# Waits of TensorE at five stage edges of a two-layer encoder step: transposes, operand order, weights, PSUM banks and evacuations

## The chip, the cores and the metric

The kernel runs on one core of a Trainium2 chip. The metric is the time of one execution on the device in microseconds, in the median of several runs. The engines of the core are TensorE (PE in the profile, with its weight loads as PEld), VectorE (DVE), ScalarE (ACT), GpSimd (POOL) and SyncE (SP), which issues most of the DMAs. Each engine works through its own instructions in a fixed order and waits on semaphores for the others.

## The reference

One inference step of a two-layer encoder with D_MODEL = 1024, on 1024 prompt tokens and 32 sample tokens, all in float32. Layer 0 mixes tokens with a state-space model (SSD), layer 1 with latent attention; after each mixer comes a gated per-layer embedding.

```python
for i in range(DEPTH):                       # DEPTH = 2
    hn_p = rmsnorm(hp, ln_w[i]); hn_s = rmsnorm(hs, ln_w[i])
    if i % 2 == 0:
        yp, cp, sp = ssd_mixer(hn_p, conv0, h0, CHUNK, *w)
        ...
    else:
        yp, lp, rp = mla_mixer(hn_p, None, None, 0, *w)
        ...
    hp = hp + yp
    hp = hp + ple(hp, p_prompt[i], ple_up_w[i], ple_norm_w[i], ple_gate_w[i])

def ssd_mixer(...):
    proj = hn @ in_w
    z, xbc, dt = jnp.split(proj, [...])      # 2048, 4096 and 32 columns
    xbc = silu(causal_conv(xbc)); dt = softplus(dt + dt_bias)
    y, hT = ssd_scan(xs, dt, A, Bm, Cm, h0, chunk)
    y = rmsnorm_by_group((y + D * xs) * silu(z))
    return y @ out_w, ...

def ple(h, p, up_w, norm_w, gate_w):
    g = jax.nn.sigmoid(rmsnorm(h, norm_w) @ gate_w)
    return (p @ up_w) * g
```

The mixer of layer 1 projects the normed input to a query latent, a key and value latent, a rotary key and a gate (`mla_in_w`), normalises the latents, attends, multiplies by the gate and projects back (`mla_out_w`).

## The kernel before

Tokens lie in the free dimension, features in the 128 partitions. A float32 product is made of three products in the faster fp32r type: each operand is split into a rounded part (h) and the rest (l), and `gemm` (L239) sums wh·ah + wh·al + wl·ah for each block of 128 features, the k-blocks, in one PSUM bank. `load_weight` (L192) fetches a weight by SP, makes wh on ScalarE (L204) and wl on GpSimd (L205); `split` (L256) does the same for an operand on ScalarE (L258) and VectorE (L259).

The program is written with tile pools: a tile waits for its buffer, and a planner puts each engine's instructions in order by a timeline that it simulates, among those that are ready the one that stands first in the program. So the written order is a priority, and an instruction that stands later can be put ahead.

The stages and the places that matter:

- **Layer 0, heads** (`phase_ssd`, L301). The 1060 columns are treated in three pieces of 384, 384 and 292 (`TILES1`). For each piece `mblock` (L341) forms the products of three head blocks, dt (32 rows), B and C. Their results go to PSUM tiles `mm`, of which there are three; one bank each is kept for the tags trx, trb, st, yd and yf (pool `ps_c`). `raw_block` (L366) forms one further block of 128 rows with `mblock`, 72 products; its results are copied out by VectorE (L362, first piece) and ScalarE (L360).
- **dt** (L431 to L483). A chain on VectorE makes `stk` out of the dt rows (dt, its running sum, and decays); nine transposes on TensorE (L482) turn it to token rows, in banks yd, yf and st, from which VectorE copies it to `tokT` (L483). After that the pool is closed, and the pool `work` of the scan takes its place.
- **Scan** (L639 to L661). For each of 8 groups: `scan_group`, the B and C blocks of the next group, the z gates of the group before, the x blocks of the next (`x_block`), and `finish`. The transposes, products and element-wise steps of the scan use `tokT`.
- **Up products** (`up_product`, L267). For layer 0 they are formed at the end of the scan stage with weights for four blocks at a time (nb = 4): 8 blocks of 3 pieces of 352 columns, each summed in an `mm` bank by six matmuls and copied to `upe` by ScalarE (L290). For layer 1 they are formed beside the attention with nb = 1.
- **Output projections** (`phase_out`, L706), for layer 0 with 16 k-blocks and for layer 1 with 8. The 1056 columns are two halves of 528 (`HB`). For each half the operands are loaded by SP (L714, five buffers `yraw`) and split (`yhl`); then 8 blocks of 128 rows are formed. `gemm2` (L675) makes both quarters (a = 0 and 1, 264 columns, a bank each) of one half: all k-blocks for a = 0, then all for a = 1. A weight covers 8 k-blocks. The operand buffers hold about one half of layer 0, so those of the second half fall free as the first half's last products are done.
- **Gated embedding** (`phase_ple`, L759) and **input of the attention** (`phase_mla_in`, L797) use `gemm2` in the same way. The operands of the latter are what `phase_ple` gives out by `emit0` (L1468), block after block and for each half; the first block of the latter starts before the last ones are there.

## Time and profile before

| | us |
|---|---|
| median of 3 runs | 1997.85 |
| lowest and highest | 1994.87 and 1999.12 |
| the profiled execution | 1996.68 |
| its span, first to last instruction | 1994.9 |

The profile's page gives each engine's busy time, a timeline in 40 slices, the DMA queues, the chain that ended last, and the costliest groups of instructions. The trace behind it answers further questions: who waited for whom, the instructions of one engine in order of time, or busy time in chosen windows. In a group or a timeline row, `out<-in` are the program's names, and `[1.32 <-ACT raw L360]` says that the engine was idle for 1.32 us just before, until ScalarE's instruction of line 360 that writes `raw` was done. In rows by windows each engine's busy time is followed by its number of instructions, and the columns at the end are the granted clock of TensorE (1.00 is full), the share of the DMA engines and GB/s. A row that merges several instructions shows the start of the first, the time to the end of the last, and their count. Matmuls are pipelined: the pace is the distance of starts, and the time shown of one is longer.

### The profile page before, as it was taken

The page shows a single profiled execution, that of the slowest core. Times are in us where ns is not written, and L with a number is a line of the kernel's source. Part 1 is how long each engine was busy: PE and PEld are TensorE (multiplying, and loading weights), DVE is VectorE, ACT ScalarE, POOL GpSimd, SP SyncE. Part 2 cuts the span into 40 slices and gives each one's busy share as a digit, 9 for nine tenths or more (in the row PEclk, how much of TensorE's full clock was granted, in tenths as well). Part 3 has the DMA queues.
Part 4 walks back from the last instruction along what each step waited for, and adds up shares of the span by engine and source line. Part 5 has one row for each costly group of instructions (what it writes and reads, how often), then busy time and mean ns, then how long its engine had stood idle before and what let it go on. Part 6 is the DMA issues. An engine that isn't in the chain of part 4 may idle for free. (4 is left out here: it accounts for less than half of the span.)

```text
span 1994.9 us, 32715 instructions
## 1 busy us (share of the span) xinstructions
PE 1921.6 (96%) x12811; PEld 1766.3 (89%) x12811; DVE 1254.2 (63%) x1613; ACT 1051.0 (53%) x1958; POOL 955.6 (48%) x811
## 2 busy tenths in 40 slices
PE   8999999999999999999998999998999999899999
PEld 6988899999999998989998999677778777779999
DVE  7888675746657575452377443364777887976544
ACT  5436555455545557342334341777687877754331
POOL 5642524343443545555777452124445454545772
PEclk9999999999999999999999999999999999999999
DMA  4134333424233347553233221434331311316442
GB/s 141 54 86 99 87 87 104 91 78 98 74 95 88 77 119 254 161 181 122 94 125 113 84 73 69 160 107 129 78 79 43 80 40 38 121 45 199 123 130 71
DMA packets 110730, 204.26 MB, mean 102 GB/s; under 512 B 18224, under 2 KB 60720, under 8 KB 110448
## 3 DMA queue, kind: packets, MB, share of 16 engines
q1 hardware_dynamic: 105472, 193.17, 33.0%
q0 software_dynamic: 2800, 6.91, 1.8%
q8 instruction: 100, 1.64, 0.3%
q10 hardware_dynamic: 2304, 2.10, 0.3%
q14 instruction: 54, 0.44, 0.1%
HBM read 156.81 MB, written 38.83 MB: 98 GB/s over the span
## 5 line engine op out<-in xcount | busy, mean ns | idle before, releaser
L205 POOL TENSOR_TENSOR wl<-wraw,wh 128x1024 fp32r<-128x1024 f32 (+3 forms) x183 | 373.4, 2042 | 424.0 <-ACT wh L204 386.2
L245 PE MATMUL mm<-hh,wl 128*128 128x384 f32 (+1 forms) x1136 | 372.7, 328 | 0.0
L245 PE MATMUL mm<-hh,wh 128*128 128x384 f32 (+1 forms) x1136 | 372.0, 328 | 0.0
L245 PE MATMUL mm<-hl,wh 128*128 128x384 f32 (+1 forms) x1136 | 370.8, 326 | 0.0
L245 PE MATMUL pso<-yhl,wh 128*128 128x264 f32 x1536 | 282.2, 285 | 4.7 <-DVE yhl L259 2.9
L204 ACT ACTIVATE wh<-wraw 128x1024 fp32r<-128x1024 f32 (+3 forms) x181 | 157.2, 869 | 245.8 <-PE pso L245 111.6
L245 PEld LDWEIGHTS pso<-yhl,wh 128*128 128x128 f32 x1536 | 238.5, 188 | 6.2 <-DVE yhl L259 4.0
L245 PE MATMUL pso<-yhl,wl 128*128 128x264 f32 x768 | 218.6, 285 | 3.9 <-POOL wl L205 3.9
L245 PEld LDWEIGHTS mm<-hh,wh 128*128 128x128 f32 x1136 | 214.6, 189 | 3.2 <-issue 2.8
L245 PEld LDWEIGHTS mm<-hl,wh 128*128 128x128 f32 x1136 | 214.8, 189 | 1.3 <-issue 0.5
L245 PEld LDWEIGHTS mm<-hh,wl 128*128 128x128 f32 x1136 | 214.6, 189 | 0.7 <-issue 0.2
L496 DVE SCALAR_TENSOR_TENSOR cx<-raw,pv,cx 128x1060 f32<-128x1060 f32 x96 | 142.6, 1490 | 42.6 <-ACT cx L494 42.0
L245 PE MATMUL psi<-yhl,wh 128*128 128x264 f32 x832 | 154.7, 287 | 4.1 <-ACT yhl L258 3.7
L559 ACT ACTIVATE ex<-ex,tokT 128x128 f32<-128x128 f32 (+1 forms) x288 | 87.0, 380 | 132.9 <-DMA ex<-acs_d 123.8
L245 PEld LDWEIGHTS pso<-yhl,wl 128*128 128x128 f32 x768 | 144.5, 188 | 4.6 <-POOL wl L205 4.6
L245 PE MATMUL pg<-hH,wl 128*128 128x264 f32 x512 | 145.9, 285 | 1.3 <-POOL wl L205 1.3
L245 PE MATMUL pg<-hH,wh 128*128 128x264 f32 x512 | 145.9, 285 | 0.0
L245 PE MATMUL pg<-hL,wh 128*128 128x264 f32 x512 | 145.6, 285 | 0.0
L1327 PE MATMUL st<-qk 128*128 128x512 f32 (+2 forms) x576 | 139.6, 358 | 1.5 <-DMA qk<-mr 0.9
L245 PEld LDWEIGHTS psi<-yhl,wh 128*128 128x128 f32 x832 | 130.7, 190 | 5.1 <-ACT yhl L258 3.9
L1348 POOL TENSOR_TENSOR pl<-pf,ph 128x512 fp32r<-128x512 f32 x64 | 81.8, 1278 | 104.7 <-DVE ph L1347 93.8
L572 POOL TENSOR_TENSOR hm<-hT,cd_all 128x256 f32<-128x256 f32 x64 | 53.1, 830 | 162.3 <-DVE hT L574 96.1
(539 smaller groups left out, 4666.5 us busy)
## 6 DMA issues: line engine op xcount, KB each, us to landing
wraw<-in_inW SPq DMA_DIRECT2D x48, 512.0 KB, 3.5
ex<-acs_d SPq DMA_DIRECT2D x32, 512.0 KB, 5.5
wraw<-in_outW SPq DMA_DIRECT2D x32, 512.0 KB, 3.7
yraw<-y_d SPq DMA_DIRECT2D x32, 264.0 KB, 4.6
u<-u_d SPq DMA_DIRECT2D x32, 264.0 KB, 2.8
eb<-ea_d SPq DMA_DIRECT2D x64, 128.0 KB, 4.0
y_d<-y SPq DMA_DIRECT2D x16, 512.0 KB, 2.8
wraw<-in_gateW SPq DMA_DIRECT2D x16, 512.0 KB, 3.6
```

The lines of the kernel that those rows point to most:

```text
L204: nc.scalar.activation(wh, raw, AF.Copy)
L205: nc.gpsimd.tensor_tensor(wl, raw, wh.bitcast(F32), op=ALU.subtract)
L245: c.nc.tensor.matmul(ps, ww[:, k, :m], aa, start=first and k == 0 and i == 0, stop=last and k == n - 1 and i == 2)
L496: nc.vector.scalar_tensor_tensor(xh, raw[:, k : k + T1], pvc(c, "cw", 4 * b + k), xh, op0=ALU.mult, op1=ALU.add)
L559: nc.scalar.activation(e_, e_, AF.Relu, scale=-1.0, bias=tok(32)[:, i, h : h + 1])
L572: nc.gpsimd.tensor_tensor(hm.rearrange("p (h q) -> p h q", q=64), hT.rearrange("p (h q) -> p h q", q=64), bc_last(cd_all[:, hs, ch], 64), ...
L1327: nc.tensor.matmul(ps[:, :n], a_[:, ks], b_[:, q], start=t == 0, stop=t == 2)
L1348: (nc.gpsimd if idx in L_POOL else nc.vector).tensor_tensor(pl[:, :n], pf[:, :n], ph[:, :n].bitcast(F32), op=ALU.subtract)
```

## The change

Five edits:

1. `mblock` takes a list of tags. The head blocks of the second piece (j = 1) use the banks of yd, yf and trb in place of the `mm` tiles.
2. The nine transposes of `stk` get an edge for the planner alone, without a semaphore: they are put in order behind the last product of the block `x_block(1, 1)`. For that `gemm` returns its last matmul, and `mblock` notes it in `c.product`.
3. `up_product` copies the middle one of the three pieces to `upe` on VectorE where nb > 1, which holds for layer 0.
4. `gemm2` takes turns: for each k-block the three products of quarter 0, then the three of quarter 1.
5. `phase_out` loads the weights of the second half's first block (k-blocks 0 to 7) ahead of that half's operands in the program.

```diff
 def gemm(...):
         for i, (ww, aa) in enumerate(((wh, a), (wh, b), (wl, a))):
-            c.nc.tensor.matmul(ps, ww[:, k, :m], aa, start=first and k == 0 and i == 0, stop=last and k == n - 1 and i == 2)
+            p = c.nc.tensor.matmul(ps, ww[:, k, :m], aa, start=first and k == 0 and i == 0, stop=last and k == n - 1 and i == 2)
+    return p
...
 def up_product(...):
-            nc.scalar.activation(u[:, w_ * a : w_ * a + w_], ps[:, :w_], AF.Copy)
+            if nb > 1 and a % 2:
+                nc.vector.tensor_copy(u[:, w_ * a : w_ * a + w_], ps[:, :w_])
+            else:
+                nc.scalar.activation(u[:, w_ * a : w_ * a + w_], ps[:, :w_], AF.Copy)
...
-    def mblock(*blocks, ws=None, js=range(3), products=gemm):
+    def mblock(*blocks, ws=None, js=range(3), products=gemm, tags=None):
...
-            for w, (_, m, evac) in zip(ws, blocks):
-                ps = mm.tile([P, 512], F32, tag="mm", name="mm")
+            for i, (w, (_, m, evac)) in enumerate(zip(ws, blocks)):
+                ps = pc.tile([P, 512], F32, tag=tags[i], name="mm") if tags else mm.tile([P, 512], F32, tag="mm", name="mm")
...
-                    products(c, ps[:, :n], w, acts, slice(0, n))
+                    c.product = products(c, ps[:, :n], w, acts, slice(0, n))
...
     for j in range(3):
-        mblock(*heads, ws=early, js=(j,), products=gemm if j else gemm_rest_last)
+        mblock(*heads, ws=early, js=(j,), products=gemm if j else gemm_rest_last,
+               tags=("yd", "yf", "trb") if j == 1 else None)
...
+        steps = []
...
-                nc.tensor.transpose(ps[:, i], stk[:, o : o + L], c.ident[:96, :96])
+                p = nc.tensor.transpose(ps[:, i], stk[:, o : o + L], c.ident[:96, :96])
+                steps.append(p.ins)
...
             x_block(g + 1, 1)
+            if g == 0:
+
+                for p in steps:
+                    tc.add_manual_dep(p, c.product.ins.name, mybir.DependencyInfo(
+                        mybir.DependencyClass.NoSync, mybir.DependencyReason.DATA), reason="late operand")
...
-def gemm2(c, ps, w, acts, kofs=0, nk=None, m=P, first=True, last=True):
-    for a in range(2):
-        gemm(c, ps[:m, a, :264], w, acts, slice(264 * a, 264 * a + 264), m, first, last)
+def gemm2(c, ps, w, acts, first=True, last=True):
+
+    n = len(acts)
+    for k in range(n):
+        for a in range(2):
+            gemm(c, ps[:, a, :264], [x[:, k : k + 1] for x in w], acts[k : k + 1], slice(264 * a, 264 * a + 264),
+                 first=first and k == 0, last=last and k == n - 1)
...
 def phase_out(...):
         acts = []
+        ws = {}
+        if hf:
+            ws[0] = load_weight(c, W[0][:, :8], 8, P)
         for k in range(nkb):
...
-        ws = {}
-
         def part(m, a, b):
 
             u = a // 8 * 8
-            if a == u:
+            if a == u and (a or m not in ws):
                 ws[m] = load_weight(c, W[m][:, u : u + 8], 8, P)
```

## The prediction

> **What bounds the kernel now.** I read the page first, then the waits of TensorE, then its timeline around each wait, and last the other engines there.

> ```profile
> span 1994.9 us, 32715 instructions
> PE 1921.6 (96%) x12811; PEld 1766.3 (89%) x12811; DVE 1254.2 (63%) x1613; ACT 1051.0 (53%) x1958; POOL 955.6 (48%) x811
> ```

> TensorE (PE) is busy 1921.6 us of the 1994.9 us span. The change removes no product, so it can win only idle time, 73 us in all, and time at a lowered clock. The waits, cut to the rows that the edits can touch (us in total, times, longest):

> ```profile
> PE pso L245 <- POOL wl L205: 3.9, 3, 1.4
> PE pstk L482 <- issue: 3.9, 1, 3.9
> PE psi L245 <- ACT yhl L258: 3.7, 1, 3.7
> PE mm L245 <- ACT upe L290: 3.0, 2, 1.5
> PE pso L245 <- DVE yhl L259: 2.9, 3, 1.5
> PE mm L230 <- ACT raw L360: 1.3, 1, 1.3
> ```

> That is 18.7 us, the most that could be won from idle time. The clock adds to it (TensorE's busy time and matmuls first, granted clock behind POOL's column):

> ```profile
> 28.40:31.80 3.40, 1.61 (x8) 1.02 (x8) 3.40 (x5) 1.60 (x4) 2.46 (x2) 1.00 0.00 0
> 31.90:35.20 3.30, 3.30 (x13) 3.06 (x12) 2.39 (x5) 2.07 (x5) 1.84 (x2) 0.50 0.01 2
> 127.50:130.80 3.30, 3.30 (x16) 3.30 (x15) 2.86 (x7) 0.34 (x1) 0.00 (x0) 0.50 0.70 137
> 1086.70:1090.00 3.30, 3.30 (x15) 3.30 (x16) 2.62 (x2) 2.63 (x5) 3.30 (x2) 0.50 0.26 79
> ```

> After each stretch with much waiting the clock is at half for about 3.4 us, in which half the work gets done: 1.7 us lost each time. Two such stretches follow waits that the change attacks, at 127.5 and 1086.7.

> **The price of the new order of products.** `gemm2` now changes the PSUM bank after every three matmuls. Its products come from the code: 1536 and 768 in the two `phase_out`, 1488 in the two `phase_ple`, 1248 in `phase_mla_in`, together 5040. The nearest rows are the head blocks, where three tiles in three banks take turns (36 to 43 us), and an ordinary block of the same 384 columns (54 to 61 us); the third row gives the pace at 264 columns:

> ```profile
> 36.00:43.00 7.00, 7.00 (x42) 6.48 (x41) 7.00 (x10) 3.29 (x7) 5.46 (x6) 1.00 0.00 1
> 54.00:61.00 7.00, 7.00 (x42) 7.00 (x42) 5.09 (x4) 4.95 (x6) 5.48 (x11) 1.00 0.46 150
> 810.00:850.00 40.00, 40.00 (x332) 40.00 (x332) 15.81 (x10) 12.77 (x17) 22.45 (x11) 1.00 0.43 138
> ```

> 42 matmuls in 7 us both ways: I take no price. The rows can't tell one matmul in 42, that is 0.17 us / 42 = 4 ns for each, and 4 ns x 5040 = 20 us is the other end; below nothing there is no reason for one. The pace at 264 columns is 40.00 / 332 = 0.1205 us. Number and size of products and weight loads stay the same.

> **Head blocks (banks): 1.3 us.**

> ```profile
> 45.28 0.35 PE L230 MATMUL mm<-hh,whl 128*64 128x292 f32 x1 [1.32 <-ACT raw L360]
> 44.80 1.83 POOL L339 TENSOR_TENSOR hl<-hf,hh 128x292 fp32r<-128x292 f32 x2 [0.88 <-ACT hh L338]
> ```

> The third piece waits 1.32 us for a bank that ScalarE still reads. With the second piece in yd, yf and trb the third finds the three mm banks of the first piece, read long before; yd, yf and trb have no other user until the x blocks. Next late would be the last two `hl`, done at 46.63; 16 of 64 products (the two last operands of three blocks) need them, the rest cover that. The evacuations move with it, so VectorE's dt chain does too. I take 1.3; bounds 0.8 (a wait for `hl` appears) and 1.3.

> **Transposes: 4.0 us.**

> ```profile
> 126.10 0.94 PE L482 MATMUL pstk<-cst,stk 96*128 96x96 f32 x9 [3.93 <-issue]
> 126.82 0.42 PE L245 MATMUL mm<-hh,wl 128*128 128x384 f32 x1
> 131.82 0.34 PE L245 MATMUL mm<-hh,wh 128*128 128x384 f32 x1
> 124.74 1.25 DVE L477 TENSOR_TENSOR stk<-w,stk 32x1060 f32<-32x1060 f32 x1
> 132.98 1.28 ACT L559 ACTIVATE ex<-ex,tokT 128x128 f32<-128x128 f32 x4 [5.14 <-DMA ex<-acs_d]
> 150.00:205.00 55.00, 51.15 (x357) 47.30 (x356) 47.94 (x58) 34.21 (x74) 17.11 (x16) 1.00 0.40 91
> ```

> "issue" hides a wait: `stk` is finished at 124.74 + 1.25 = 125.99, and TensorE, which had nothing else first in its order, starts at 126.10. Behind the nine transposes stand the last 25 matmuls of the x block that the edit names (between the rows at 126.82 and 131.82, one of 384 columns and 24 of 292; by the 810 row in proportion to the columns 0.175 and 0.133 us): 3.4 us. They now go ahead, so the wait shrinks from 3.9 to about 0.5, and with that little idle time the half clock at 127.5 goes: 3.4 + 1.7 = 5.1 us. The transposes themselves keep their time, since they still wait for `stk`; all that is queued behind them (the copies to tokT on VectorE, the ex loads on SP, for which ScalarE then waits to 132.98) isn't later. But nor is it earlier, and from 150 to 205 TensorE is idle 3.85 us in waits on that scan. Work pulled ahead may be lacking there. I take 4.0, between 1.7 (only the clock stays won) and 5.1.

> **Evacuation of the up products: 1.4 us.**

> ```profile
> 762.44 1.28 ACT L182 ACT_TABLE_LOAD   x1
> 763.74 1.18 ACT L182 ACTIVATE yr<-yr,eps 128x1060 f32<-128x1060 f32 x1
> 765.35 0.80 ACT L290 ACTIVATE upe<-mm 128x352 f32<-128x352 f32 x2
> 766.17 1.28 ACT L183 ACT_TABLE_LOAD   x1
> 768.59 2.56 DVE L622 SCALAR_TENSOR_TENSOR y<-y,pv,yr 128x1060 f32<-128x1060 f32 x2 [2.24 <-ACT yr L183]
> ```

> Both 1.5 us waits come while ScalarE works at a table load and a long function, and three full banks wait. With every third tile read by VectorE the first wait loses the 0.4 us of one copy (0.80 / 2), as its next tile is ScalarE's; at the second one bank more is free, six matmuls (0.9 us) of slack, so 0.4 + 1.0. Two thirds of the copies stay where they were. The new copies wait in VectorE's queue: behind the L622 above, itself late by 2.24 us, one would gain nothing. Bounds 0 and 3.0.

> **Second half of the first output projection: 2.5 us.**

> ```profile
> 876.21 2.39 POOL L205 TENSOR_TENSOR wl<-wraw,wh 128x1024 fp32r<-128x1024 f32 x1 [1.66 <-ACT wh L204]
> 884.88 1.04 ACT L204 ACTIVATE wh<-wraw 128x1024 fp32r<-128x1024 f32 x1
> 888.42 0.39 PE L245 MATMUL pso<-yhl,wl 128*128 128x264 f32 x1 [1.40 <-POOL wl L205]
> 894.75 0.39 PE L245 MATMUL pso<-yhl,wh 128*128 128x264 f32 x1 [1.51 <-DVE yhl L259]
> 888.86 6.46 DVE L259 TENSOR_TENSOR yhl<-yraw,yhl 128x528 fp32r<-128x528 f32 x5
> 898.83 0.71 DVE L748 TENSOR_TENSOR hf<-pso,xres 128x528 f32<-128x528 f32 x1 [3.51 <-PE pso L245]
> ```

> The last of 16 operands is done at 888.86 + 6.46 = 895.32. Then 27 matmuls were left, 3 of the first half and 24 of the second; by turns six are left. 21 x 0.1205 = 2.5 us. The weights moved ahead are those of k-blocks 0 to 7. Their `wl` was done at 878.60, and they are in use for 48 matmuls (5.8 us) before the wait that ends at 888.42: they were on time, and moving them is worth nothing here. In the planner's order their load goes ahead of 16 operand loads in SP's queue, their copy and subtraction ahead of 16 copies on ScalarE and the sums on POOL; they need a weight buffer that falls free only as the first half ends, so I expect the same places as now, and if SP did wait for that buffer, the operand loads behind it would slip (rival 1). That wait is for k-blocks 8 to 15, whose `wh` (884.88) stands in ScalarE's queue between operand copies. Copies could now come earlier, as operand slots fall free evenly; then up to 4.5. If the planner puts that `wh` behind more copies, the gain is eaten: 0. In the other `phase_out` the late operand is a part of its own, six matmuls either way: nothing.

> **First block of the attention's input: 2.5 us.**

> ```profile
> 1085.81 0.39 PE L245 MATMUL psi<-yhl,wh 128*128 128x264 f32 x1 [3.73 <-ACT yhl L258]
> 1091.35 1.05 PE L694 MATMUL n<-acc,ones 128*128 128x264 f32 x4
> 1094.32 0.71 DVE L259 TENSOR_TENSOR yhl<-u,yhl 128x528 fp32r<-128x528 f32 x1 [0.71 <-ACT yhl L258]
> 1098.24 0.28 PE L245 MATMUL psi<-yhl,wl 128*128 128x264 f32 x1
> ```

> The eighth operand of the first half comes at 1085.8. Again 21 matmuls go ahead (2.5 us), the wait falls to 1.2, and the half clock at 1086.7 (1.7) should go: the operand's lower part follows 0.7 us behind, six matmuls take another 0.7, and the first half ends near 1087.2 instead of 1091.35. Next late is the second half's eighth operand, at 1094.32 + 0.71 = 1095.03: 42 matmuls reach to 1092.3, a new wait of 2.7 follows, and the half ends at 1095.8 instead of 1098.4: 2.6, rounded to 2.5. Bounds 0.9 (the new wait draws a half clock of its own) and 4.2. [...]

> **Sum.** 1.3 + 4.0 + 1.4 + 2.5 + 2.5 = 11.7 us. The profiled execution took 1996.68 us, its span and 1.8 us around it, so 1985.0; the median of the runs is 1.2 higher, 1997.85, and so my forecast is 1986. Upper ends together give 18.1, so 1979.8, and the range begins at 1979.

> **Rivals.** (1) The next link takes it back: 1.3 + 1.7 + 0 + 0 + 0.9 = 3.9, 1994. For it speaks the idle VectorE-paced stretch from 150 to 205; against it, that TensorE gets ahead in products that it must do anyway.

> (2) The planner, which orders every engine by its own timeline, orders something else worse.

> ```profile
> 1250.00:1798.00 548.00, 517.72 (x2570) 407.59 (x2569) 390.80 (x670) 401.56 (x854) 241.90 (x273) 0.99 0.30 83
> ```

> The attention is idle 30.3 us; a third more is 10, total 1996. Against it: no edit lies there.

> (3) Slower: the change of banks costs. It decides from 11.7 us / 1680 changes = 7 ns; at the 4 ns per matmul that the rows can't exclude, 20 - 11.7 = 8 us slower, 2006. For it speaks nothing but that limit.

> (4) The alternation lowers the clock: 5040 x 0.1205 = 607 us are some 178 windows; if one in ten ran at half, 18 x 1.7 = 30 us, 2016. [...] Against it the 36 to 43 row, with three banks and a clock of 1.00.

> (5) The planner's late edge or the early weights do nothing. For the weights this is the forecast; for the transposes the total would be 1990.

> **How the numbers follow.** Forecast 0.58 (1979 to 1993), (1) 0.20, (2) 0.11, (3) 0.05, (4) 0.02, (5) 0.04. A measurement of this kernel can tell about 0.2%, 4 us. Faster: 0.58, half of (1), and (5): 0.72. Same: half of (1) and most of (2): 0.18. Slower: 0.10. The range 1979 to 1995 leaves out (3), (4), most of (2) and a little of the rest.

> **What would show it.** The waits of pstk (under 1 us) and mm<-raw (gone); x-block products before L482; no half clock near 127 and 1087; pso<-yhl shorter by 2.5 us, pso<-wl still there; a new wait of psi for the second half's operand; the pace at 264 columns still 0.1205. Wrong would be: a pace above 0.122, more idle time from 133 to 260 than before by over 3 us, or a changed total from 1250 to 1798.

## The result, and the profile after

| | us |
|---|---|
| before, median of 5 runs | 1997.85 (1994.87 to 2000.80) |
| after, median of 5 runs | 1986.9 (1983.91 to 1987.96) |
| ratio, with its 95% interval | 0.9943 (0.9929 to 0.9958) |
| the profiled execution after | 1987.96, its span 1986.2 |

The kernel became 11.4 us faster by the ratio. 1986 was forecast. But the terms of the sum came out otherwise than forecast, and their errors cancelled, which is luck; most of what follows is about that.

The head of the page after:

```profile
span 1986.2 us, 32717 instructions
PE 1919.2 (97%) x12811; PEld 1763.4 (89%) x12811; DVE 1257.4 (63%) x1621; ACT 1047.6 (53%) x1950; POOL 957.9 (48%) x811
```

TensorE does the same 12811 matmuls. The waits of TensorE (us in total, times, longest), cut to the rows that the edits touch:

```profile
PE pso L245 <- POOL wl L205: 3.9, 4, 1.3
PE pg L245 <- POOL wl L205: 3.0, 1, 3.0
PE n L710 <- POOL acc L703: 2.6, 1, 2.6
...
PE mm L245 <- ACT upe L294: 2.3, 2, 2.1
...
PE mm L245 <- DVE upe L292: 2.0, 2, 1.7
```

The wait for the `wl` of k-blocks 8 to 15 is there as before. The wait for `raw` is gone, that for the operands of `pso` is down to 0.2 us, and that of `psi` to 0.56. New is a wait for VectorE's copies. Two waits grew: that of the norm's products for a sum on GpSimd (0.4 before), and that for a `wl` in the gated embedding (1.3 before). TensorE's timeline at the places of the five edits:

```profile
45.35 0.32 PE L231 MATMUL mm<-hl,whl 128*32 128x292 f32 x1 [0.24 <-DVE hl L343]
123.53 0.30 PE L245 MATMUL mm<-hh,wl 128*128 128x292 f32 x1
124.41 0.93 PE L488 MATMUL pstk<-cst,stk 96*128 96x96 f32 x9 [0.58 <-PE mm L245]
764.97 0.59 PE L245 MATMUL mm<-upx,wh 128*128 128x352 f32 x2 [2.06 <-ACT upe L294]
885.48 0.39 PE L245 MATMUL pso<-yhl,wl 128*128 128x264 f32 x1 [1.18 <-POOL wl L205]
1086.50 0.39 PE L245 MATMUL psi<-yhl,wh 128*128 128x264 f32 x1 [0.21 <-ACT yhl L259]
1087.25 0.39 PE L245 MATMUL psi<-yhl,wh 128*128 128x264 f32 x1 [0.35 <-DVE yhl L260]
1090.73 1.58 PE L710 MATMUL n<-acc,ones 128*128 128x264 f32 x4 [2.62 <-POOL acc L703]
```

In the head pieces only the forecast wait for an `hl` is left (0.24). The transposes come behind the x block and wait 0.58 in place of 3.93. At 1087 the eighth operand hardly stops TensorE, but 0.9 us later it stands for 2.62 us until the squares are summed. Windows around two of the waits (TensorE's busy time first, granted clock behind POOL's column):

```profile
224.40:227.70 3.30, 1.49 (x11) 1.40 (x10) 0.72 (x2) 0.00 (x0) 0.00 (x0) 1.00 0.11 36
227.80:231.10 3.30, 3.30 (x17) 2.80 (x17) 3.12 (x6) 3.22 (x10) 1.01 (x3) 0.50 0.43 109
1088.00:1091.30 3.30, 0.68 (x4) 0.50 (x4) 0.71 (x1) 1.20 (x3) 3.30 (x3) 1.00 0.00 0
1091.40:1094.70 3.30, 3.30 (x15) 3.10 (x14) 0.71 (x1) 1.48 (x3) 0.00 (x0) 0.50 0.45 159
```

The half clock at 127 is gone, but there is one at 227.8, in the scan; and the one of 1087 came 5 us later, behind the longer wait for the sum.

### The profile page after: what moved, and what is told of

Read it like the earlier page. It is cut to its first block, busy times and chain, and to the rows that moved or that the text cites. A ratio compares the mean times of both kernels' runs of the same rounds, so it can differ in the third digit from the quotient of the medians.

```text
span 1986.2 us, 32717 instructions
## 1 busy us (share of the span) xinstructions
PE 1919.2 (97%) x12811; PEld 1763.4 (89%) x12811; DVE 1257.4 (63%) x1621; ACT 1047.6 (53%) x1950; POOL 957.9 (48%) x811
## 3 DMA queue, kind: packets, MB, share of 16 engines
q8 instruction: 100, 1.64, 0.3%
## 5 line engine op out<-in xcount | busy, mean ns | idle before, releaser
L205 POOL TENSOR_TENSOR wl<-wraw,wh 128x1024 fp32r<-128x1024 f32 (+3 forms) x183 | 374.0, 2045 | 405.2 <-ACT wh L204 383.7
L245 PE MATMUL mm<-hh,wl 128*128 128x384 f32 (+1 forms) x1136 | 372.0, 328 | 0.0
L245 PE MATMUL mm<-hh,wh 128*128 128x384 f32 (+1 forms) x1136 | 371.4, 327 | 0.0
L245 PE MATMUL mm<-hl,wh 128*128 128x384 f32 (+1 forms) x1136 | 369.4, 325 | 0.0
L245 PE MATMUL pso<-yhl,wh 128*128 128x264 f32 x1536 | 281.2, 285 | 0.2 <-DVE yhl L260 0.2
L204 ACT ACTIVATE wh<-wraw 128x1024 fp32r<-128x1024 f32 (+3 forms) x181 | 157.1, 869 | 235.2 <-PE pso L245 103.0
L245 PEld LDWEIGHTS pso<-yhl,wh 128*128 128x128 f32 x1536 | 237.7, 188 | 0.4 <-DVE yhl L260 0.4
L245 PE MATMUL pso<-yhl,wl 128*128 128x264 f32 x768 | 218.2, 284 | 3.9 <-POOL wl L205 3.9
L245 PEld LDWEIGHTS mm<-hh,wh 128*128 128x128 f32 x1136 | 213.8, 188 | 3.5 <-issue 3.2
L245 PEld LDWEIGHTS mm<-hl,wh 128*128 128x128 f32 x1136 | 214.2, 189 | 0.7 <-issue 0.2
L245 PEld LDWEIGHTS mm<-hh,wl 128*128 128x128 f32 x1136 | 213.9, 188 | 0.9 <-issue 0.2
L566 ACT ACTIVATE ex<-ex,tokT 128x128 f32<-128x128 f32 (+1 forms) x288 | 87.3, 380 | 139.3 <-DMA ex<-acs_d 129.9
L245 PE MATMUL psi<-yhl,wh 128*128 128x264 f32 x832 | 154.5, 287 | 0.6 <-DVE yhl L260 0.4
L245 PEld LDWEIGHTS pso<-yhl,wl 128*128 128x128 f32 x768 | 144.9, 189 | 5.0 <-POOL wl L205 5.0
L245 PE MATMUL pg<-hH,wl 128*128 128x264 f32 x512 | 145.6, 284 | 3.0 <-POOL wl L205 3.0
L245 PE MATMUL pg<-hH,wh 128*128 128x264 f32 x512 | 146.1, 285 | 0.0
L245 PE MATMUL pg<-hL,wh 128*128 128x264 f32 x512 | 145.7, 285 | 0.0
L245 PEld LDWEIGHTS psi<-yhl,wh 128*128 128x128 f32 x832 | 130.0, 190 | 1.8 <-DVE yhl L260 0.6
```

What stands on the lines that cost most here:

```text
L204: nc.scalar.activation(wh, raw, AF.Copy)
L205: nc.gpsimd.tensor_tensor(wl, raw, wh.bitcast(F32), op=ALU.subtract)
L245: p = c.nc.tensor.matmul(ps, ww[:, k, :m], aa, start=first and k == 0 and i == 0, stop=last and k == n - 1 and i == 2)
L566: nc.scalar.activation(e_, e_, AF.Relu, scale=-1.0, bias=tok(32)[:, i, h : h + 1])
```

## The clock's grid, and why one profile misleads

Before the experiments, what all of them need. A half-clock window is a stretch in which the granted clock is 0.50. Those of all fourteen profiles are 3.41 us long or a multiple of it (where the end of a profile does not cut them), and within one run they lie on one grid of 3.41 us. The grid stands differently to the program in each run: windows begin at 31.84 us in the profile before and at 227.75 in the one after, 57.4 stretches apart. Cut along it, the fourteen traces give 8047 stretches at full clock. Where TensorE was busy for less than 45% of the stretch, the next was at half clock in 56 of 56 cases; from 45 to 55% in 25 of 54; from 55 to 60% in 0 of 61; above that in 9 of 7876. So in these traces the clock goes by the busy share of a fixed stretch, with the limit between 0.45 and 0.55. The nine are exceptions: eight lie in the attention, in stretches with the transposes `pq` or the products `pz` (the busiest at a share of 0.83); why, no trace shows.

By these counts a wait under about 1.5 us (45% of 3.41, an estimate), if no other falls into the same stretch, costs its own length. A longer one may also cost the work that a half-clock window loses, or not, by where the grid lies. In the window at 1086.6 in the profile before, products of 264 columns start 0.220 us apart in place of 0.122, so a window loses about 1.5 us (3.41 x (1 - 0.122 / 0.220)), not the 1.7 of the prediction. The kernels lost 3 to 17 us to such windows in one profile each. Two profiles of one stage can therefore differ by some us without a cause in the kernel. So I compare each stage over all fourteen profiles, those with the edit against those without:

| stage (first matmul to first matmul) | edit | with: mean (n) | without: mean (n) | difference, ± two standard errors | forecast |
|---|---|---|---|---|---|
| start to the first ordinary block | 1 | 52.29 (8) | 55.70 (6) | -3.4 ± 0.9 | -1.3 |
| from there to the up products | 2 | 700.73 (8) | 703.96 (6) | -3.2 ± 1.2 | -4.0 |
| up products | 3 | 29.31 (6) | 29.58 (8) | -0.3 ± 0.5 | -1.4 |
| first output projection | 4 | 191.33 (7) | 194.86 (7) | -3.5 ± 1.0 | -2.5 |
| gated embedding and input of the attention | 4 | 273.71 (5) | 272.69 (6) | +1.0 ± 1.6 | -2.5 |
| sample queries and attention | none | 542.24 (7) | 543.03 (7) | -0.8 ± 2.0 | 0 |
| second projection and gated embedding | 4 | 191.16 (7) | 191.91 (7) | -0.8 ± 0.3 | 0 |

(In the fifth row three kernels with further edits there are left out. The sixth is split by edit 4.) The differences sum to -11.0 (-10.2 without the row that no edit touches), the medians' ratio gives -11.4.

## The experiments

Totals are medians, and ratios are to the kernel before in the same set of runs (medians 1998.78, 1998.05 and 1998.92), with 95% intervals.

### Each edit alone

**The transposes alone:** `steps` and the planner's edge, as in edit 2.

> Edit 2 alone (the nine transposes ordered behind the x block). Theory: the wait of pstk falls from 3.9 us to under 1, but the work pulled ahead is missing later: the stretch from the first ordinary block to the first up product gets shorter by only 1.5 to 2.5 us, new waits of 1.5 to 2 us each appear between 133 and 260 us, and a half-clock window still falls there, only later. Total about 1995 to 1996. Rival: the edit by itself keeps its whole 4 to 5 us and it is the other edits that take it back in the changed kernel; then this stretch is shorter by 4 us or more and the total is about 1993.

1996.46 us, ratio 0.9990 (0.9981 to 0.9999). The wait fell to 0.60 us, and the stretch from the first ordinary block to the up products got 3.8 us shorter (700.42 against 704.18): close to the rival's 4, with no window in it. The theory's total fits nearly, but for another reason: the start got 3.15 us longer, in code that this edit leaves alone.

```profile
45.82 0.50 PE L230 MATMUL mm<-hh,whl 128*64 128x292 f32 x1 [2.84 <-ACT raw L361]
...
41.50:44.90 3.40, 1.48 (x9) 1.15 (x7) 3.40 (x5) 1.92 (x5) 2.90 (x3) 1.00 0.00 0
45.00:51.70 6.70, 5.88 (x24) 5.23 (x25) 1.44 (x4) 1.45 (x4) 1.83 (x2) 0.50 0.00 0
```

The wait for `raw`, 1.32 us in the profile of before, is 2.84 here, and two half-clock windows go with it.

**The turns alone:** the new `gemm2`.

> Edit 4 alone (turns of the two quarters). Theory: it carries most of the gain. First output projection shorter by 2.5 us, first block of the attention's input by 2.3, the gated embedding of layer 0 longer by 1.7 (a later wl on GpSimd), pace at 264 columns still 0.1205 us: total 1992 to 1995. Rival 1: the 1.7 us come from the weights loaded ahead; then the gated embedding is unchanged here and the total is 1991 to 1992. Rival 2: the 1.4 us that the output projection of layer 1 got shorter by come from the weights loaded ahead; then that stage is unchanged here.

1994.3 us, ratio 0.9983 (0.9972 to 0.9994). The first output projection got 2.85 us shorter, the gated embedding 0.5 shorter: the longer one of the changed kernel isn't from this edit. The last stage pair got 1.35 us shorter, so that gain is of the turns and not of the early weights (rival 2 falls). The input of the attention got 3.3 us longer, where 2.3 shorter was expected:

```profile
1085.20 0.39 PE L245 MATMUL psi<-yhl,wh 128*128 128x264 f32 x1 [2.01 <-ACT yhl L258]
1085.94 0.39 PE L245 MATMUL psi<-yhl,wh 128*128 128x264 f32 x1 [0.35 <-DVE yhl L259]
1087.14 1.81 PE L698 MATMUL n<-acc,ones 128*128 128x264 f32 x4 [0.32 <-POOL acc L691]
1098.36 2.13 PE L698 MATMUL n<-acc,ones 128*128 128x264 f32 x4 [2.66 <-POOL acc L691]
```

The operand's wait is shorter, as forecast, and what it gave comes back as a wait for the sum of squares.

**The early weights alone:** edit 5.

> Edit 5 alone (weights of the second half's first block ahead of its operands). Theory: nothing in either output projection, every stage within 0.5 us of before, the wait for the wl of k-blocks 8 to 15 (1.40 us before) still there, total 1996 to 1999. Rival: it is what shortens the output projection of layer 1 by 1.4 us, in which 8 k-blocks are the whole weight, total 1995 to 1996.5.

1999.16 us, ratio 1.0004 (0.9994 to 1.0014): nothing. More than that, every engine has the same instructions in the same order as before: the planner puts that load where it did. So this is a second profile of the same program, and shows how far two can lie apart: span 1999.4 against 1994.9, eleven half-clock windows against seven. The rows come in pairs, a stretch of waiting and what follows it:

```profile
42.90:46.30 3.40, 0.71 (x5) 0.65 (x6) 3.31 (x6) 2.74 (x7) 2.52 (x4) 1.00 0.00 0
46.40:49.70 3.30, 3.30 (x16) 3.00 (x15) 0.00 (x0) 0.00 (x0) 0.52 (x1) 0.50 0.00 0
...
889.50:892.80 3.30, 1.72 (x11) 1.45 (x11) 3.30 (x3) 3.19 (x5) 2.50 (x3) 1.00 0.29 110
892.90:899.60 6.70, 5.83 (x21) 4.84 (x21) 4.00 (x3) 3.26 (x4) 2.20 (x1) 0.50 0.87 266
```

The projection at 892.9 has two windows that the profile of before doesn't have, for 2.5 us.

**The evacuation alone:** edit 3.

> Edit 3 alone (the middle piece of the up products copied by VectorE). Theory: nothing, since the copies on VectorE wait behind the long element-wise steps there as those on ScalarE wait behind the table loads: the up stage within 0.7 us of before, waits of mm for VectorE's upe of about 2 us in place of those for ScalarE, total 1996.5 to 1999. Rival, as predicted: the stage gets shorter by 1.4 to 3 us when the scan ahead of it is as before, total 1994 to 1996.

1999.7 us, ratio 1.0009 (1.0001 to 1.0018): no gain, as the theory had it. The up stage took 29.93 us (29.56 before). Of two waits of 1.5 us one of 2.05 was left, and a half-clock window followed: up to 773.20 the products behind it start 0.29 us apart, then 0.16. The waits for VectorE's copies that the theory expected did not come in this run:

```profile
766.56 0.59 PE L245 MATMUL mm<-upx,wh 128*128 128x352 f32 x2 [0.30 <-ACT upe L293]
769.84 0.92 PE L245 MATMUL mm<-upx,wh 128*128 128x352 f32 x2 [2.05 <-ACT upe L293]
```

**The banks alone:** edit 1.

> Edit 1 alone (head blocks of the second piece in yd, yf and trb). Theory: in four runs whose head code is that of before, the wait of mm for ScalarE's raw was 2.8 to 2.9 us and a half-clock window followed at 45 to 46 us; the profile of before, with 1.3 us, was the exception, because a half-clock window at 31.84 had slowed the products ahead of the wait. So the edit is worth more than the 1.3 predicted: the first ordinary block starts at 51.5 to 52.5 us (53.95 before, 55.6 to 57.1 in the four), no wait of mm for raw, no window from 40 to 50, total 3 to 4 us under before's median. Rival, as predicted: 1.3 us.

1997.82 us, ratio 0.9997 (0.9985 to 1.0009). The first ordinary block started at 52.40 us, with no wait for `raw` and no window from 40 to 50, as expected. The total was not: 0.6 us for 3 to 4. This run has the early window of the profile of before (31.0 us), and two where before had one:

```profile
28.00:31.00 3.00, 1.21 (x6) 0.48 (x4) 3.00 (x5) 1.57 (x3) 1.95 (x3) 1.00 0.00 0
31.10:34.40 3.30, 3.30 (x10) 2.75 (x11) 2.63 (x4) 2.12 (x5) 1.72 (x2) 0.50 0.01 2
119.80:123.10 3.30, 0.92 (x6) 0.60 (x4) 3.27 (x2) 0.00 (x0) 3.30 (x2) 1.00 0.01 0
123.20:126.50 3.30, 1.85 (x11) 1.87 (x12) 3.24 (x5) 1.23 (x2) 2.16 (x7) 0.50 0.53 178
126.60:129.90 3.30, 3.30 (x16) 3.30 (x14) 2.32 (x6) 0.62 (x2) 0.00 (x0) 0.50 0.74 144
```

Against the same early window (before's start of 53.95) the edit gave 1.55 us there; against the five runs without it (55.60 to 57.10) 3.2 or more.

### Two edits, and all but one

**Banks and transposes:** edits 1 and 2.

> Edits 1 and 2 together. Alone they gave 0.6 and 2.0 us in the medians, while all five gave 11. Theory: no interplay, the gain of each depends on which of its waits draws a half-clock window in a run, and the two give 3 to 6 us, total 1992 to 1995. Rival: they need each other (each alone leaves a window in the neighbourhood of the other's wait); then they give 7 or more, total 1991 or less. The kernel with edit 5 alone issues the same instructions in the same order on every engine as the kernel before, so its 0.8 us over before's median shows how far such medians can be off.

1992.11 us, ratio 0.9962 (0.9948 to 0.9976), 7.6 us by the ratio: the median within the theory's range, the gain that of the rival. The up products start 6.0 us earlier than in the profile of before, and no window lies ahead of them. The two edits alone sum to 2.6 us by their ratios, so the pair gives 5.0 ± 4.1 more; the five single edits sum to 3.4, with an uncertainty of about 4.6, and all together gave 11.4 ± 2.9, which is 8.0 ± 5.4 more. By these totals the edits give more together than alone, as the rival has it. The profiles of the single edits point the same way: each has two half-clock windows at the wait of the other edit (45.0 to 51.7 and 123.2 to 129.9), this one has none at either place; four kernels with neither edit have one at each. That is one profile each, so how the edits are linked is not shown; the table of stages, which takes each edit by itself, cannot see such a link.

**All but the evacuation:** the line of edit 3 undone.

```diff
-            if nb > 1 and a % 2:
-                nc.vector.tensor_copy(...)
-            else:
-                nc.scalar.activation(...)
+            nc.scalar.activation(u[:, w_ * a : w_ * a + w_], ps[:, :w_], AF.Copy)
```

> All edits but edit 3 (all up products copied by ScalarE again). Theory: edit 3 is worth nothing; the total stays at 1985 to 1989 and the up stage at 29.5 to 30 us with two waits of 1.5 us for ScalarE. Rival: in the run of edit 3 alone the up stage was 1.3 us shorter once the half-clock window in it is taken off; if that holds, this kernel is slower than the changed one by 1 to 2 us, 1988 to 1990.

1987.39 us, ratio 0.9944 (0.9923 to 0.9966), as with it; the up stage took 29.59 us. Edit 3 is worth nothing that can be measured.

**The changed kernel a second time.**

> The changed kernel a second time. Theory: the grid of 3.41 us stretches by which the clock goes stands otherwise to the program in each run. So the half-clock windows lie elsewhere or in another number than in the first profile (six, 8.8 us of work lost), and the stages agree within 1 us only once that loss is taken off: 1972 to 1973 us in all without it. The wait pg<-wl of 3.1 us, which neither single edit shows, comes again if it lies in the order of instructions. Rival: the windows stay where they were, and the five edits gave all of the difference in windows.

1987.44 us, ratio 0.9943 (0.9925 to 0.9961). The windows lie elsewhere (140, 765, 1079, 1379, 1734 us). Without their loss the stages sum to 1970.5 us, 2 under the first profile, more apart than I expected. The 3.0 us wait of pg, which I took for a matter of order, is not there, though the order of instructions is the same:

```profile
1057.79 0.39 PE L245 MATMUL pg<-hH,wl 128*128 128x264 f32 x1 [1.03 <-POOL wl L205]
1070.89 0.39 PE L245 MATMUL psi<-yhl,wl 128*128 128x264 f32 x1 [1.13 <-POOL wl L205]
1077.24 0.39 PE L245 MATMUL psi<-yhl,wh 128*128 128x264 f32 x1 [1.21 <-ACT yhl L259]
1077.99 0.39 PE L245 MATMUL psi<-yhl,wh 128*128 128x264 f32 x1 [0.36 <-DVE yhl L260]
```

The embedding is 2.2 us shorter than in the first profile, the stage behind it 2.2 longer: together 272.46 in the first and 272.42 in this one (273.11 before). So most of the 2.3 us that the first profile shows as won at the input of the attention had been lost just ahead of it, in the embedding: the last operands were done at nearly the same time.

### The price of a change of bank

After all edits, the bank changes after every matmul and not after every third.

```diff
-    for k in range(n):
-        for a in range(2):
-            gemm(c, ps[:, a, :264], [x[:, k : k + 1] for x in w], acts[k : k + 1], ...)
+    for k, (ah, al) in enumerate(acts):
+        for i, (ww, aa) in enumerate(((wh, ah), (wh, al), (wl, ah))):
+            for a in range(2):
+                c.nc.tensor.matmul(ps[:, a, :264], ww[:, k, :P], aa[:, 264 * a : 264 * a + 264], ...)
```

> All edits, and gemm2 changes the bank after every matmul in place of every third: three times as many changes, 5040. Theory: a change costs nothing, the pace at 264 columns stays 0.1205 us and the clock at 1.00 in the projections, total 1985 to 1989. Rival: a change costs 4 ns (what the rows of before could not exclude); then 3360 more cost 13 us, total 2000, pace about 0.123. Rival 2: the alternation makes half-clock windows; then they are found between 790 and 1250 us.

1984.74 us, ratio 0.9940 (0.9917 to 0.9963), a little under the expected 1985 to 1989. From 900 to 960 us, in the output projection, 497 matmuls start or run, one or two more than in the kernels before and after (495 and 496):

```profile
900.00:960.00 60.00, 60.00 (x497) 60.00 (x497) 16.61 (x11) 17.25 (x22) 32.74 (x15) 1.00 0.38 117
```

Two half-clock windows lie from 790 to 1250 (1077 and 1088 us), both behind waits, so rival 2 falls too. The last gated embedding, 768 products without a wait (720 of them in the order that the edit changes), gives the price to the nanosecond: 95.35 to 95.36 us in all seven kernels without turns, 95.13 to 95.14 in all seven with them, at every third matmul or at every one. A bank change costs nothing; the new order is even 0.22 / 768 = 0.3 ns per matmul faster, for a reason that no run shows.

### Does the clock go by useful work?

In the kernel before, matmuls with zero weights are added ahead of the late operand.

```diff
+                gemm(c, ps[:, 0, :264], [x[:, :7] for x in w], acts[:7], sl, last=False)
+                for _ in range(26):
+                    nc.tensor.matmul(ps[:64, 0, :264], c.zeros_r, acts[6][0][:, sl], start=False, stop=False)
+                gemm(c, ps[:, 0, :264], [x[:, 7:] for x in w], acts[7:], sl, first=False)
```

> The kernel before, with 26 matmuls of zero weights (264 columns, 3.1 us) added to the first block of the attention's input ahead of its eighth operand; the sum does not change. Theory: the clock goes by TensorE's busy share in fixed stretches of 3.41 us, whatever it works at. The wait for the operand falls from 3.7 to 4.6 us to 0.6 to 1.6, the block waits as long as before for its operand, and the half-clock window at 1087 us, found in all six kernels with that wait, is not there; the stage from psi to the sample queries takes 175 us, 1.7 to 2 less than before's 176.9, although TensorE does 3.1 us more work. Rival: the window has another cause, so it stays, and the stage takes 177 us or more.

1994.93 us, ratio 0.9992 (0.9976 to 1.0007).

```profile
1082.69 3.36 PE L815 MATMUL psi<-yhl,zeros_r 128*64 128x264 f32 x26
1087.46 0.39 PE L245 MATMUL psi<-yhl,wh 128*128 128x264 f32 x1 [1.41 <-ACT yhl L258]
1088.20 0.39 PE L245 MATMUL psi<-yhl,wh 128*128 128x264 f32 x1 [0.36 <-DVE yhl L259]
1096.03 0.39 PE L245 MATMUL psi<-yhl,wh 128*128 128x264 f32 x1 [0.94 <-ACT yhl L258]
...
1084.50:1087.80 3.30, 1.89 (x14) 1.46 (x12) 2.02 (x3) 1.48 (x3) 0.85 (x2) 1.00 0.31 104
1087.90:1091.20 3.30, 3.00 (x24) 3.00 (x25) 2.62 (x3) 3.08 (x6) 3.18 (x2) 1.00 0.36 121
```

The window is gone, as the theory said: 1.89 of 3.30 us busy, most of it with work that is useless, keeps the clock. But the stage took 177.6 us, not 175: TensorE, now faster, waited 0.94 us for the eighth operand of the second half, the very link that the prediction named as next. From the first half's eighth operand to the second half's norm products it is 13.1 us in both kernels, and the eighth operand itself came 0.5 us later after the stage's start. Here a clock kept high ahead of late data won nothing.

### Behind the new waits

Two edits after all five: the last sum of squares goes to VectorE, and the splits of the cached latents behind the latents.

```diff
-            sumsq(c, tmp, h1, accs[hf], m == 0)
+            sumsq(c, tmp, h1, accs[hf], m == 0, c.nc.vector if m == 7 else None)
...
         def latents_done():
+            for k in range(2):
+                for a in range(2):
+                    ...
+                    split(c, st.lats[k][0][:, cols], st.lats[k][1][:, cols], raw)
```

The reason stands in the timelines of GpSimd and VectorE of the changed kernel. The sum waits behind a weight's scaling, and the last operand's `u` (L189, L810) behind three splits `lsL`:

```profile
1087.53 1.90 POOL L198 TENSOR_TENSOR wraw<-wraw,pv 128x1024 f32<-128x1024 f32 x1 [4.75 <-DMA wraw<-in_miW]
1089.39 1.29 POOL L703 TENSOR_TENSOR acc<-acc,sq 128x528 f32<-128x528 f32 x1
...
1079.18 4.75 DVE L260 TENSOR_TENSOR lsL<-lc,lsH 128x512 fp32r<-128x512 f32 x3 [0.35 <-ACT lsH L259]
1083.86 0.69 DVE L189 SCALAR_TENSOR_TENSOR u<-t,u 128x528 f32<-128x528 f32 x1
```

> The changed kernel, and behind its waits at the input of the attention two more edits: the last addition to the sum of squares by VectorE in place of GpSimd (where it stood behind the 1.90 us scaling of a weight), and the splits of the cached latents after the latents (they stood on VectorE ahead of the last operand's chain). Theory: these two are what was late there next; the waits n<-acc of 2.8 us and psi<-yhl of 0.4 and 0.6 us go, the half-clock window at 1091 with them, the stage from psi to the sample queries falls from 174.6 to 170.5 to 172 us, total 1982 to 1984. Rival: the next link (the eighth operand of the second half) takes it back, stage 173.5 or more, total as changed.

1984.34 us, ratio 0.9923 (0.9904 to 0.9942). The wait for the sum is gone, and so is the window. The operand's wait, which should have gone, is 1.20 + 0.36 us, as in the second profile of the changed kernel (1.21 + 0.36); so nothing here shows that moving the splits did anything:

```profile
1076.35 0.39 PE L245 MATMUL psi<-yhl,wh 128*128 128x264 f32 x1 [1.20 <-ACT yhl L259]
1077.09 0.39 PE L245 MATMUL psi<-yhl,wh 128*128 128x264 f32 x1 [0.36 <-DVE yhl L260]
1084.89 1.16 PE L710 MATMUL n<-acc,ones 128*128 128x264 f32 x4 [0.20 <-ACT r L182]
```

The stage took 172.9 us, above the expected 172; with the embedding ahead of it, 268.6 against 272.46 and 272.42 in the two profiles of the changed kernel. The total is just above the expected 1982 to 1984, and its interval overlaps that of the changed kernel.

**Both:** the last two kernels together.

> The kernel of e8_sum_and_splits with the bank changed after every matmul, as in e7_every_product. Theory: both gains add (2 to 4 us for the first; for the second 0 to 2, since the wl of a weight and the lower part of an operand are needed two matmuls and one later), total 1979 to 1983, the fastest here. Rival: the lower median of e7_every_product was chance, total as e8_sum_and_splits.

1981.5 us, ratio 0.9906 (0.9888 to 0.9923), the fastest here, as expected. Its interval ends just below that of the changed kernel (0.9925 to 0.9961 in the same set of runs), so this version beats the kernel before and the changed one. The embedding and the input of the attention took 271.0 us here, with a half-clock window at 1076.8.

## Why the prediction was right, point by point

- **Head blocks: right in kind, too small.** The wait goes, the next late is an `hl`, as said. 1.3 us was the wait of one profile; there a half-clock window at 31.8 had slowed the products ahead of it, which fits banks that were nearly free. In the five runs with the old code and no such window the wait was 2.8 to 2.9 and drew a window of its own. The edit measured 3.4.
- **Transposes: right.** The products of the x block go first, as forecast, the wait 0.58, the window of 127 gone in all eight kernels; 3.2 ± 1.2 for 4.0. The doubt in the text, that the work pulled ahead is missing in the scan, holds in part: the longest wait there is 1.4 to 2.2 us (1.7 before), and in three of the eight a window comes there.
- **Evacuation: wrong.** The step that failed is "the first wait loses the 0.4 us of one copy", with the second wait's 1.0. One wait for ScalarE grew to 2.1, and VectorE's copies are themselves waited for (2.0 us); a wait of the first `pso` for the last copy, which the prediction leaves out, went (first row below). -0.3 ± 0.5 for 1.4; near the lower bound of 0. The mean hides two outcomes: the stage took 29.9 us in three profiles with the edit and 28.7 to 28.8 in the three others, with the changed kernel's two profiles on both sides. In its first, one of VectorE's operand splits ahead of a copy took 2.88 us (the median of 48 is 0.71) while GpSimd worked at a `wl` from 770.81 to 773.75; in its second the two splits at that place took 1.64 together and no copy was waited for. (The rows are from before, and from the first and second profile after.)

```profile
PE pso L245 <- ACT upe L290: 1.2, 1, 1.2
...
771.43 2.88 DVE L260 TENSOR_TENSOR yhl<-yraw,yhl 128x528 fp32r<-128x528 f32 x1
...
769.24 1.64 DVE L260 TENSOR_TENSOR yhl<-yraw,yhl 128x528 fp32r<-128x528 f32 x2
```

- **First output projection: right.** 2.5 forecast, 2.6 in the first profile, 3.5 ± 1.0 over all, as two of the kernels without turns have two half-clock windows each there (196.5 us, the others 194.0 to 194.5). The early weights are worth nothing, as said, and the wait for k-blocks 8 to 15 stays (1.18).
- **Input of the attention: wrong, though the first profile seemed to confirm it.** The step that failed is "Next late is the second half's eighth operand". The operand's wait fell as worked out, but the next late thing was the sum of squares on GpSimd, 2.5 to 3.2 us at its longest in all five kernels with turns and no further edit there, not the second half's operand. That one is next only once the clock stays up (the run with zeros). Over all, no gain of the turns shows there: +1.0 ± 1.6 for -2.5.
- **The second projection, "nothing":** 0.8 ± 0.3 with the last embedding. 0.2 of it is the new order's pace in the embedding, and the 768 products of the projection would give as much again (an estimate by that pace). The late operand and its lower part added 0.45 to 1.3 us to the pace in the seven profiles without turns and 0.35 to 1.0 in the seven with them, on average 0.2 less.
- **Price of a bank change: right at nothing.** "Below nothing there is no reason for one" was wrong: -0.3 ns per matmul.
- **Rivals.** The next link took the gain back at two places of five, the input of the attention and the up products (1). The attention did not change (2), a change of bank costs nothing (3) and draws no window (4); that one stretch in ten would run at half clock was an assumption, which no run shows. Of (5), the early weights do nothing, and the late edge works.
- **The signs.** Of the three that the prediction calls wrong none came: the pace at 264 columns is 0.121 us from 900 to 960 in both kernels, TensorE is idle for 6.8 us from 133 to 260 (5.6 before), and the attention is the same within ± 2.0. Two of the expected signs failed: half clock still came near 1087 (at 1091.3), and the new wait was for the sum, not for the second half's operand.

So the total was right because errors cancelled, and that is luck: two terms were too small (head by 2.1, first projection by 1.0) and one was missing (0.8), three were too large (input of the attention by 3.5, evacuation by 1.1, transposes by 0.8), and the attention gave 0.8 that no edit explains and its ± 2.0 covers. The errors of the first projection and of the transposes are no larger than their uncertainty. That the edits seem to give more together than alone stands against adding up terms at all, and is open.

## What to carry to other kernels

Read a wait of TensorE together with the 3.41 us stretch that it lies in: where less than 45% of one was busy, a half-clock window followed here in 56 of 56 cases and cost up to 1.5 us more, and whether a wait does so differs from run to run. So take a wait's size from several profiles, and a stage's gain together with the stage ahead of it: two profiles of one program gave 2.2 us more in the one and as much less in the other. Turns of products ahead of late data won where nothing else was late behind them (first projection, 3.5 us); where the next link was as late they only moved the wait (input of the attention, +1.0 ± 1.6 us), and there the chain that makes the data has to be ordered first.
